# A mixer block's first stage: TensorE in a written order, whole modulations, one load queue

## The chip, the cores and the metric

The kernel runs on one core of one Trainium2 chip. TensorE (PE in the profile) multiplies matrices, VectorE (DVE), ScalarE (ACT) and GpSimd (POOL) work on elements, SyncE (SP) mostly issues transfers; ACT and POOL can issue transfers too. The metric is the device time of one execution in microseconds (us). Before the change it is 1306.2 us, the median of 3 runs (1304.97 to 1307.42).

## The reference

One layer of a diffusion block over 512 latent tokens with 2048 channels, and 256 context tokens. The input is normalised and modulated by a shift and a scale that come from a conditioning vector; one wide projection feeds an attention branch and a Fourier branch; both are gated, projected, merged and added to the input.

```python
shift, scale, gate = jnp.split(silu_c @ w_ada[l] + b_ada[l], 3, axis=-1)
h = _modulate(_rmsnorm(xs, norm_g[l]), shift[:, None], scale[:, None])
p = h @ w_l                      # q, k, v, z_a, u_b, z_b, g_a, g_b
...
y_a = (attn * jax.nn.silu(z_a)) @ w_pa
y_b = (_fourier_mix(u_b) * jax.nn.silu(z_b)) @ w_pb
out = xs + gate[:, None] * ((g_a * y_a + g_b * y_b) @ w_o)
```

`_fourier_mix` is the real part of a two-dimensional FFT over the tokens and over the 128 channels of each of four groups. All is float32; the kernel multiplies in a reduced float32 by writing each operand as a high and a low half and taking three products.

## The kernel before

The channels are cut into 16 input blocks of 128 (`kb` 0 to 15). x is held transposed (`xt`, channels by tokens).

**First stage** (lines 453 to 653). It computes the Fourier branch's two inputs: u_b, four tiles of 128 channels (tiles 0 to 3), and z_b, four more (tiles 4 to 7), each by 512 tokens. For every input block it needs three things:

- a *modulation* (`modulation`, L584): the block's 128 shifts and 128 scales, a product of the conditioning vector with 2 MB of `w_ada`, loaded in two halves of 1 MB (tag `wada`, four buffers, so two blocks). The product runs in four strips of 32 columns of TensorE (`matvec`, L527; the rows of line 534, 32 records to a modulation), ACT copies it out (`ado`, L542), TensorE transposes it twice (L545), DVE sums it to columns (L551) and makes `shift` and `gain` (L590, L591);
- the *rows* of the modulated input (`make_h`, L519): DVE multiplies by the gain and the norm (L521), ACT adds the shift and rounds to the high half (L522), DVE takes the low half (L523);
- the block's *weights* (`w_start`), loaded in pieces of up to 512 KB (`STEPS`, L41: one block with eight tiles for blocks 0 to 3, then two blocks with four tiles) and split into halves by ACT and DVE (`split_piece`, L254, whose two instructions are lines 177 and 178). Four raw buffers and three pairs of halves hold them; two more raw buffers (`mr`) serve from block 8 on.

A tile's product with a block is three matmuls (`mm3`, L326: high by high, line 328; high by low, line 329; low by high, line 330). The u tiles add up over all blocks in four PSUM banks of their own and are copied out once at the end; the z tiles go piece by piece through two other banks and are added on DVE into `part` (`keep`, L564; ACT for block 0). `start_work` (L559) is a generator that issues these products. The loop at L612 issues a modulation, the rows, then products that are due. The order of instructions on each engine is not the written one: a scheduler with a cost model of its own places what is ready, except inside `manual_schedule`, where the written order holds, and with `issue_after`, which keeps an instruction behind a given one on its engine. Before, only the modulations from block 3 on are inside `manual_schedule`, each for itself.

From block 8 on `form_row` (L601) makes two further forms of the input rows for the later products.

*Loads.* x, the first pieces and the modulations 0 to 2 are issued by SP; modulations from block 3 on by POOL (L462); the later pieces and the transform's tables by ACT (`asks`), at blocks given by `ASK`; pieces are split at blocks given by `SPLIT`.

**Transform** (lines 655 to 727). The Fourier mix is matrix products: `channels` with a table of 128 by 256 (`fch`), `positions` with tables of sines and cosines (`fsq`, two halves of 512 KB raw). The tables are split into halves after the first stage, `halves` forms sums and differences of u, `gate_b` applies SiLU to z, and each `positions` result is multiplied into z. The last four products of the first stage (z tiles, blocks 12 to 15) are issued in the same stretch.

**Afterwards** come the other projections, in products of a seven-product scheme (`Group`), attention, the branch projections and the output projection. Their weights come through the same queue of pieces: `get` (L287) hands out the next and splits as many ahead as `look` says, 4 from the end of the first stage, bounded by the pairs of halves (three, and two more from the group's second product, Q5).

Of the kernel before, what the change touches and what calls it, by code (L numbers as in the profile page):

```python
# [18 lines left out]
P = 128  # L19
# [24 lines left out]

ASK, SPLIT, MORE_RAW = (*range(1, 9), 9, 9, 10, 10, 11, 12), (*range(2, 13), 14), 8
# [75 lines left out]
def block_kernel(ctx, tc, xT, ctx_rows, ctx_toks, x, c_row, w_ss, w_gate, vecs, qkg, rope, dft_c, dft_s,  # L121
# [76 lines left out]
    def start_load():  # L198
# [12 lines left out]
        for p, src in zip(free, e.parts):  # L211
            raw = p[0].tile([P, 1024], F32, tag=p[2], bufs=p[3], name=uid("wr"))[:, : e.cols]
            asks[0].dma_start(raw if len(src.shape) == 2 else raw.rearrange("p (i j c) -> p i j c", i=4, j=2), src)
            e.raws.append((p, raw))
# [7 lines left out]
    may, asks = [0], [nc.sync]  # L222
# [134 lines left out]
    for p in start_pieces():  # L357
        if p[2:5:2] == (KK - 4, 4):
            for q in range(2):
                stream(("dfts", q), dft_s[:, q], 1024, 2, "raw")  # L360
            stream(("dftc", 0), dft_c, 256, 1, "raw")
        stream(("start", p), w_start[p[0] : p[0] + P * p[1]].rearrange("(p c) -> p c", p=P), p[1], p[2 + 1])
# [94 lines left out]
    mr, mrp = region("mr")  # L457
    xt = pap.tile([P, KK, T], F32, name="xt")

    def wada_load(kb, h):  # L460
        w = pap.tile([P, 8, 256], F32, tag="wada", bufs=4, name=uid("wa"))
        (nc.gpsimd if kb > 2 else nc.sync).dma_start(w, w_ss[kb, :, 8 * h : 8 * h + 8, :])  # L462
        return w

    for a, n in XCH:
        nc.sync.dma_start(xt[:, a : a + n, :], xT[:, a : a + n, :])


# [4 lines left out]
    nc.scalar.activation(ce, cvt, ACT.Exp, scale=-1.0)  # L473
    nc.scalar.activation(rt, ce[:, 0:1], ACT.Sqrt)
# [4 lines left out]
                            ce.rearrange("p (j k) -> p j k", j=2), op=ALU.mult)  # L479
    def token_norms():  # L480
# [30 lines left out]
    wada = {(0, h): wada_load(0, h) for h in range(2)}  # L511
    may[0] = 3
    load_more()
    wada.update({(1, h): wada_load(1, h) for h in range(2)})
    may[0] = 1
    load_more()
    asks[0] = nc.scalar

    def make_h(hi, lo, src, rr, kb, j):  # L519
        tmp = src  # L520
        first = nc.vector.scalar_tensor_tensor(tmp, src, gain[:, kb, j : j + 1], rr, op0=ALU.mult, op1=ALU.mult)  # L521
        act = nc.scalar.activation(hi, tmp, ACT.Identity, bias=shift[:, kb, j : j + 1])  # L522
# [36 lines left out]
    def start_work():  # L559
# [7 lines left out]
        for p in start_pieces():  # L567
            kb, nk, t, nt = p[2:]
            if (kb, t) == (KK - 4, 4):
                yield 0  # L570
# [1235 lines left out]
```

## Time and profile before

| | |
|---|---|
| median of 3 runs | 1306.2 us (1304.97 to 1307.42) |
| profiled execution | 1305.55 us, of which the span of the profile is 1303.3 us |
| granted TensorE clock, mean | 0.998 |
| busy: PE, PEld, DVE, ACT, POOL | 1279.5, 1047.4, 995.1, 685.4, 180.6 us |
| first matmul of the first stage's tiles | 23.47 us from the start |
| first matmul of the first product after the transform | 169.39 us |
| bytes moved | 318.54 MB, mean 244 GB/s |

The profile is one execution. Times run from the start of its span. A row of the timeline gives the start, the length, the engine, the line of the kernel, the operation, output and inputs by the names in the program, the shape, the count, and in brackets how long the engine had been idle and what released it. A matmul's row is longer than its share of the array, since matmuls overlap: what counts is the distance between starts. PEld is the weight load, which overlaps the matmul. A name such as `s` stands for a slot tile (rows of the input), `whi` and `wlo` for the halves of a weight piece, `pb` for the banks of the u tiles and of the transform, `pc` for those of the z tiles, `pd` for those of the modulations.

### The profile page before, as it was taken

The page shows a single profiled execution, that of the slowest core. Times are in us where ns is not written, and L with a number is a line of the kernel's source. Part 1 is how long each engine was busy: PE and PEld are TensorE (multiplying, and loading weights), DVE is VectorE, ACT ScalarE, POOL GpSimd, SP SyncE. Part 2 cuts the span into 40 slices and gives each one's busy share as a digit, 9 for nine tenths or more (in the row PEclk, how much of TensorE's full clock was granted, in tenths as well). Part 3 has the DMA queues.
Part 4 walks back from the last instruction along what each step waited for, and adds up shares of the span by engine and source line. Part 5 has one row for each costly group of instructions (what it writes and reads, how often), then busy time and mean ns, then how long its engine had stood idle before and what let it go on. Part 6 is the DMA issues. An engine that isn't in the chain of part 4 may idle for free.

```text
span 1303.3 us, 17544 instructions
## 1 busy us (share of the span) xinstructions
PE 1279.5 (98%) x6522; PEld 1047.4 (80%) x6522; DVE 995.1 (76%) x1295; ACT 685.4 (53%) x1079; POOL 180.6 (14%) x244
## 2 busy tenths in 40 slices
PE   6999999999999999999999999999999999999997
PEld 3577888888888888888888888888888888888885
DVE  4666899979688887657687766688798867887676
ACT  5222655555556465444254554666666646464544
POOL 0110011110202111011021010011110212221210
PEclk9999999999999999999999999999999999999999
DMA  9898487887899988976879897468872899998985
GB/s 382 338 373 349 178 244 183 242 243 255 209 284 260 265 287 271 292 209 179 273 200 267 294 224 258 169 221 245 251 230 82 236 246 250 244 212 232 220 205 173
DMA packets 103718, 318.54 MB, mean 244 GB/s; under 512 B 9808, under 2 KB 33104, under 8 KB 99280
## 3 DMA queue, kind: packets, MB, share of 16 engines
q0 software_dynamic: 30288, 123.75, 40.4%
q1 hardware_dynamic: 48720, 163.65, 35.3%
q10 hardware_dynamic: 24624, 30.02, 6.6%
q8 instruction: 51, 0.84, 0.2%
q14 instruction: 35, 0.29, 0.1%
HBM read 283.30 MB, written 34.09 MB: 244 GB/s over the span
## 4 chain that ended last, share of the span: by engine, by line
PE 91%; DMA 3%; DVE 2%; ACT 2%; issue 1%; SPq 0%; ACTq 0%; DVEq 0%
PE banks L328 10%; PE banks L329 10%; PE banks L330 10%; PE x L328 9%; PE x L330 9%; PE x L329 9%; PE y L329 7%; PE y L328 7%; PE y L330 7%; PE pd L534 2%; PE banks L1294 2%; PE pb L328 2%; PE pb L330 2%; PE pb L329 2%; DMA wa<-in_w_ss 1%; PE pc L328 1%
## 5 line engine op out<-in xcount | busy, mean ns | idle before, releaser
L177 ACT ACTIVATE whi<-R 128x1024 fp32r<-128x1024 f32 x138 | 145.2, 1059 | 140.2 <-PE banks L330 47.3
L178 DVE TENSOR_TENSOR wlo<-R,whi 128x1024 fp32r<-128x1024 f32 x138 | 167.5, 1221 | 55.4 <-ACT whi L177 55.2
L178 DVE TENSOR_TENSOR wlo<-wr,whi 128x1024 fp32r<-128x1024 f32 (+1 forms) x123 | 148.5, 1212 | 63.4 <-ACT whi L177 63.2
L177 ACT ACTIVATE whi<-wr 128x1024 fp32r<-128x1024 f32 (+1 forms) x123 | 128.8, 1051 | 116.6 <-PE y L330 37.4
L328 PE MATMUL banks<-whi,s 128*128 128x512 f32 x396 | 157.1, 397 | 2.2 <-DVE ev L862 1.5
L330 PE MATMUL banks<-whi,s 128*128 128x512 f32 x396 | 155.2, 392 | 0.0
L329 PE MATMUL banks<-wlo,s 128*128 128x512 f32 x396 | 155.1, 392 | 0.0
L328 PE MATMUL x<-whi,s 128*128 128x512 f32 x352 | 137.2, 390 | 0.0
L330 PE MATMUL x<-whi,s 128*128 128x512 f32 x352 | 137.0, 389 | 0.0
L329 PE MATMUL x<-wlo,s 128*128 128x512 f32 x352 | 137.0, 389 | 0.0
L328 PE MATMUL y<-whi,s 128*128 128x512 f32 x316 | 123.1, 389 | 0.4 <-DVE cxe L1015 0.4
L329 PE MATMUL y<-wlo,s 128*128 128x512 f32 x316 | 123.1, 390 | 0.3 <-DVE wlo L178 0.3
L330 PE MATMUL y<-whi,s 128*128 128x512 f32 x316 | 122.8, 389 | 0.0
L281 POOL DMA_DIRECT2D R<-in_w_g x64 | 55.9, 874 | 420.2 <-DVE wlo L178 247.5
L177 ACT ACTIVATE s<-wr 128x512 fp32r<-128x512 f32 (+2 forms) x93 | 60.4, 676 | 68.6 <-DMA wr<-cf_d 21.8
L178 DVE TENSOR_TENSOR s<-wr,s 128x512 fp32r<-128x512 f32 (+2 forms) x93 | 66.8, 749 | 31.7 <-ACT s L177 30.9
L328 PEld LDWEIGHTS banks<-whi,s 128*128 128x128 f32 x396 | 74.4, 188 | 17.7 <-ACT whi L177 1.9
L330 PEld LDWEIGHTS banks<-whi,s 128*128 128x128 f32 x396 | 74.4, 188 | 15.5
L329 PEld LDWEIGHTS banks<-wlo,s 128*128 128x128 f32 x396 | 74.4, 188 | 14.0 <-DVE wlo L178 0.2
L330 PEld LDWEIGHTS x<-whi,s 128*128 128x128 f32 x352 | 66.1, 188 | 13.8
L329 PEld LDWEIGHTS x<-wlo,s 128*128 128x128 f32 x352 | 66.1, 188 | 13.6
L328 PEld LDWEIGHTS x<-whi,s 128*128 128x128 f32 x352 | 66.1, 188 | 13.6
(293 smaller groups left out, 2829.4 us busy)
## 6 DMA issues: line engine op xcount, KB each, us to landing
wr<-in_w_g SPq DMA_DIRECT2D x128, 512.0 KB, 5.2
R<-in_w_g POOLq DMA_DIRECT2D x64, 512.0 KB, 7.5
wa<-in_w_ss POOLq DMA_DIRECT2D x26, 1024.0 KB, 8.2
R<-in_w_g SPq DMA_DIRECT2D x32, 512.0 KB, 5.6
wr<-in_w_gate SPq DMA_DIRECT2D x32, 512.0 KB, 5.1
wr<-in_w_o SPq DMA_DIRECT2D x24, 512.0 KB, 7.7
R<-in_w_o POOLq DMA_DIRECT2D x24, 512.0 KB, 9.5
wr<-in_w_pab SPq DMA_DIRECT2D x20, 512.0 KB, 6.4
```

The costliest lines, as they stand in the source:

```text
L177: first = nc.scalar.activation(hi, src, ACT.Copy)
L178: return first, nc.vector.tensor_tensor(lo, src, hi.bitcast(F32), op=ALU.subtract)
L281: nc.gpsimd.dma_start(chain[e.pc], e.nxt, accum_op=ALU.add)
L328: nc.tensor.matmul(o, ah, bh, start=start, stop=False, skip_group_check=cont)
L329: nc.tensor.matmul(o, ah, bl, start=False, stop=False, skip_group_check=cont)
L330: nc.tensor.matmul(o, al, bh, start=False, stop=stop, skip_group_check=cont)
L534: last = nc.tensor.matmul(acc[32 * j : 32 * j + 32, :256], c2[:, 8 * h + k, :], w[:, k, :], start=n < 4, stop=n >= KK - 4)
L1294: nc.tensor.transpose(tp[:, k * P : (k + 1) * P], p[:, k * P : (k + 1) * P], ident)
```

## The change

- All of TensorE's instructions from the norms to the transform's last tile stand in `manual_schedule`. Each modulation is written whole between two tiles: for blocks 0 to 3 two tiles, the next modulation, two tiles, its transposes, four tiles; then two modulations to a pair of blocks. The copy (ACT) is issued with the modulation (`modulate`), the transposes and the columns later (`columns`); the gain is made before the shift.
- Within a piece of two blocks the u tiles go by block first, then by tile. Where a piece has eight tiles, u and z tiles alternate (`TURNS`).
- All loads of the stage are issued by SP, chained in the written order (`ask`, `load_start`): after a modulation is written, the one two blocks later (three for the first) and the next piece are asked for. POOL and ACT issue none of them. The two raw buffers `mr` are gone; `ASK`, `SPLIT` and `MORE_RAW` too. Before the second modulation's load stand two pieces instead of three.
- The first sine table (`fsq0`) and the channel table (`fch`) have tiles beside `part`, are loaded before block 12's first piece and split after block 13's rows, in the loop's turn `kb == 10`. The second sine table is split after the stage.
- Each split of a piece, and each `form_row`, is kept behind the rows of the block at which it stands. The sums and differences of u are kept behind the last additions to the first z tiles.
- One, two and three of the next pieces are split between the transform's tiles; `look` is 2 after the transform and 4 from Q5 of the first group on.
- The square-root function is first called on a constant right behind the exponential.

The diff, cut to its core:

```diff
-ASK, SPLIT, MORE_RAW = (*range(1, 9), 9, 9, 10, 10, 11, 12), (*range(2, 13), 14), 8
+TURNS = (0, 4, 1, 5, 2, 6, 3, 7)
...
+        if p[2:5:2] == (KK - 4, 0):
+            stream(("dfts", 0), dft_s[:, 0], 1024, 2, "raw")
             stream(("dftc", 0), dft_c, 256, 1, "raw")
+        elif p[2:5:2] == (KK - 4, 4):
+            stream(("dfts", 1), dft_s[:, 1], 1024, 2, "raw")
...
-    def wada_load(kb, h):
-        w = pap.tile([P, 8, 256], F32, tag="wada", bufs=4, name=uid("wa"))
-        (nc.gpsimd if kb > 2 else nc.sync).dma_start(w, w_ss[kb, :, 8 * h : 8 * h + 8, :])
-        return w
...
+    def ask(q, *a):
+        with ExitStack() as line:
+            if last_load[0] is not None and q is nc.sync:
+                line.enter_context(tc.issue_after(last_load[0]))
+            ins = q.dma_start(*a).ins
+        if q is nc.sync:
+            last_load[0] = ins
...
+    def load_start():
+        may[0] = 1
+        with tc.issue_after(last_load[0]):
+            load_more()
+        assert not may[0]
+        last_load[0] = asked[0].ins
...
+    for n in range(len(XCH)):
+        load_x(n)
+    wada = {0: wada_load(0)}
+    for _ in range(2):
+        load_start()
+    wada[1] = wada_load(1)
+    load_start()
...
+    def modulate(kb):
+        two[kb] = bank2()
+        for h in range(2):
+            matvec(kb, h)
+        o = o_of[kb] = pap.tile([P, 256], F32, tag="ada_o", bufs=2, name=uid("ado"))
+        wada.pop(kb)
+        return nc.scalar.copy(o, two[kb][:, :256])
...
+            order = [[(i, k) for k in range(nk)] for i in range(nt)]
+            if t == 0 and nk > 1:
+                order = [[(i, k)] for k in range(nk) for i in range(nt)]
+            elif nt == 8:
+                order = [order[i] for i in TURNS]
...
+    with tc.manual_schedule(engines={mybir.EngineType.PE}):
+        norms = token_norms()
+        modulate(0)
+        wada[2] = wada_load(2)
+        load_start()
+        columns(0)
+        ins = make_h(0)
+        nc.scalar.copy(rx, rx0[0])
+        split_next()
+        with behind(ins):
+            split_next()
+            split_next()
+        for kb in range(4):
+            some(2)
+            modulate(kb + 1)
+            if kb < 3:
+                wada[kb + 3] = wada_load(kb + 3)
+                load_start()
+            some(2)
+            columns(kb + 1)
+            ins = make_h(kb + 1)
+            with behind(ins):
+                split_next()
+            if kb == 3:
+                some(2)
+                modulate(5)
+                for k in (6, 7):
+                    wada[k] = wada_load(k)
+                    load_start()
+                some(2)
+                columns(5)
+                make_h(5)
+            else:
+                some(4)
+        for kb in range(4, KK - 2, 2):
+            n = 3 if kb < KK - 4 else 2
+            for i in range(2):
+                k = kb + 2 + i
+                some(n)
+                modulate(k)
+                if k + 2 < KK:
+                    wada[k + 2] = wada_load(k + 2)
+                    for _ in range(2 if k + 2 == KK - 3 else 1):
+                        load_start()
+                some(2 - i)
+                columns(k)
+                ins = make_h(k)
+                with behind(ins):
+                    split_next()
+                    if k >= 8:
+                        form_row(k - 8)
+                if k == KK - 2:
+                    load_start()
+            some(n - (n == 2))
+            with behind(ins):
+                if kb == KK - 6:
+                    split_table(0)
+                    split_from(get(("dftc", 0)), fch[:, 0, :], fch[:, 1, :])
+                    load_start()
+        some(8)
...
-    for q in range(2):
-        split_from(get(("dfts", q)).rearrange("p (m n) -> p m n", m=2), fsq[:, 0, q], fsq[:, 1, q])
-    raw = get(("dftc", 0))
-    split_from(raw, fch[:, 0, :], fch[:, 1, :])
-    for g in range(4):
-        halves(g)
+    ordered = ExitStack()
+    ordered.enter_context(tc.manual_schedule(engines={mybir.EngineType.PE}))
+    for n in range(4):
+        next(work)
+        if n < 2:
+            with behind((finals[-1],)):
+                halves(2 * n)
+                halves(2 * n + 1)
...
         positions(g)
         if g < 2:
             channels(g + 2)
+        with behind((finals[-1],)):
+            for e in ahead[:g]:
+                split_piece(e)
+    ordered.close()
+    look[0] = 2
...
             if (g, name) == (0, "Q5"):
                 hl_pools += range(MORE_HL)
+                look[0] = 4
```

`some(n)` issues the next n steps of `start_work`, each a tile of a piece (a tile and a block for the u tiles of a two-block piece); `behind(ins)` is `issue_after` for several instructions.

More of the change, by code (lines that the diff above doesn't have):

```diff
@@ L509, in spread @@
         return acc
[L511 to L522, printed above, removed]
-        second = nc.vector.scalar_tensor_tensor(lo, tmp, shift[:, kb, j : j + 1], hi.bitcast(F32),
-                                                op0=ALU.add, op1=ALU.subtract)
-        return first, second, act
```

199 lines of the change are left out of this document (92 added, 107 removed).

## The prediction

> **What bounds the kernel now.** I read the page first, then a table of stretches with the edges put where TensorE changes its kind of work, then TensorE's own timeline in the first stretches.
>
> ```profile
> span 1303.3 us, 17544 instructions
> ...
> 0.00:23.47 23.47, 13.32 (x64) 6.53 (x65) 11.64 (x28) 15.10 (x27) 1.90 (x11) 1.00 0.93 368
> 23.47:63.00 39.53, 38.97 (x269) 23.37 (x270) 23.29 (x42) 10.16 (x17) 5.56 (x10) 1.00 0.91 357
> 63.00:137.95 74.95, 74.90 (x567) 52.92 (x567) 49.24 (x99) 22.13 (x32) 8.61 (x16) 1.00 0.86 337
> 137.95:169.39 31.44, 31.18 (x204) 28.49 (x204) 29.23 (x46) 19.64 (x31) 0.54 (x1) 1.00 0.57 205
> 169.39:400.00 230.61, 230.61 (x1020) 191.01 (x1019) 200.79 (x240) 128.72 (x223) 33.86 (x38) 1.00 0.86 241
> ```
>
> The stretch rows give the stretch, its length, then busy time and count for PE, PEld, DVE, ACT and POOL, the granted clock, the DMA share and GB/s. They are: the load of x and the norms; the input blocks 0 to 5; blocks 6 to 15; the end of the first stage with the transform; and the first of the products that follow. TensorE looks full in all but the first, but busy time says little here (a matmul's row is 0.39 us long while the next starts 0.23 us after it), so I count instructions. In the last row 1020 matmuls take 230.61 us, 0.2261 us each: nothing to gain there. For the stage itself I need the pitch of its matmuls, of a modulation, and of one that is cut:
>
> ```profile
> 48.13 0.40 PE L330 MATMUL pc<-s,wlo 128*128 128x512 f32 x1
> 48.46 0.62 PE L534 MATMUL pd<-wa,c 128*32 128x256 f32 x2
> 49.01 0.50 PE L328 MATMUL pc<-s,whi 128*128 128x512 f32 x1
> 49.35 0.40 PE L329 MATMUL pc<-s,whi 128*128 128x512 f32 x1
> ...
> 49.91 1.06 PE L534 MATMUL pd<-wa,c 128*32 128x256 f32 x12
> ...
> 51.79 1.48 PE L534 MATMUL pd<-wa,c 128*32 128x256 f32 x18
> ...
> 59.87 1.93 PE L534 MATMUL pd<-wa,c 128*32 128x256 f32 x30
> ...
> 88.23 0.39 PE L330 MATMUL pc<-s,wlo 128*128 128x512 f32 x1
> 88.55 1.93 PE L534 MATMUL pd<-wa,c 128*32 128x256 f32 x32
> 90.42 0.50 PE L328 MATMUL pc<-s,whi 128*128 128x512 f32 x1
> 90.75 0.40 PE L329 MATMUL pc<-s,whi 128*128 128x512 f32 x1
> 91.22 0.38 PE L545 MATMUL pd<-ident,ado 128*128 128x128 f32 x2
> 91.67 0.39 PE L329 MATMUL pc<-s,whi 128*128 128x512 f32 x1
> ...
> 163.03 0.28 PE L329 MATMUL pb<-fch,uh 128*128 128x256 f32 x1
> 163.15 0.28 PE L330 MATMUL pb<-fch,ul 128*128 128x256 f32 x1
> ```
>
> The pitch of a plain matmul I take as 0.2275 us (between the steady 0.2261 above and the 0.23 to 0.24 between starts here). A whole modulation (32 records) costs 88.23 to 90.75, 2.52 us, less two pitches: 2.07 us. The two transposes cost 91.22 to 91.67, 0.45, less one pitch: 0.22; with the short step into them I use 0.25. Now count. The stretch 23.47 to 63.00 holds 269 records: five modulations (160), ten transposes, so 99 matmuls. Ideal: 99 x 0.2275 + 5 x 2.07 + 5 x 0.25 = 34.1 us, measured 39.5: **5.4 us lost**. The stretch 63.00 to 137.95 holds ten modulations and 227 matmuls: 51.6 + 23.2 = 74.8 against 74.95, 0.1 lost. In 137.95 to 169.39 there are 144 matmuls of the transform (four times 12 and 24), which start 0.12 apart (163.03, 163.15), and 60 others: 13.7 + 17.3 = 31.0 against 31.44, 0.5 lost (about the wait quoted further down). So at most 6.0 us (0.46%) can be won between 23.47 and 169.39, and the start before that is bound by transfers at 0.93 of the DMA engines.
>
> **The change part by part.**
>
> *Whole modulations.* Modulations 1 to 5 are cut today, the later ones are whole. Two are cut 16 + 16 (1.07 us each by their rows below), two 2 + 30, one 2 + 12 + 18.
>
> ```profile
> 25.28 1.07 PE L534 MATMUL pd<-wa,c 128*32 128x256 f32 x16
> 27.66 1.07 PE L534 MATMUL pd<-wa,c 128*32 128x256 f32 x16
> ```
>
> A cut of two records costs 48.13 to 49.35, 1.22 us, less two pitches, 0.76 us, all of it extra, since the 30 left take the same 1.93 as 32. Halves cost 2 x 1.07 - 1.93 = 0.21 and one more entry and exit, each 0.1 (88.23 to 88.55 and 90.42 to 90.75 against 0.2275): 0.42. The 12 + 18 cost 1.06 + 1.48 - 1.93 + 0.21 = 0.82. Sum: 2 x 0.42 + 3 x 0.76 + 0.82 = **3.9 us** that a whole modulation saves. Six extra pieces in all.
>
> The Trainium skill ("TensorEngine Tiling (Array Packing)", section Key Properties) says that a change of tiling mode drains TensorE; a modulation works in strips of 32 columns and the rest in the full array, so it would charge each extra piece two drains. If the drains, the 0.21 us of entry and exit, were all that a cut costs, six would be worth 1.3 us and not 3.9. The trace charges more, because the 2-record rows are 0.62 long where two of 32 should be 0.12.
>
> *The written order's own waits.* TensorE now takes tiles, modulation and transposes as written, so where a scheduler today fills a wait with another tile, it will stand. Of the 5.4 us lost, 1.5 are waits that exist already (5.4 - 3.9). New ones come from this chain (DVE, ACT and PE rows of block 4, and of block 0):
>
> ```profile
> 23.45 0.75 DVE L523 SCALAR_TENSOR_TENSOR s<-xt,shift,s 128x512 fp32r<-128x512 f32 x1 [0.33 <-ACT s L522]
> 23.47 1.20 PE L328 MATMUL pb<-s,whi 128*128 128x512 f32 x4 [0.30 <-ACT s L522]
> ...
> 45.83 0.38 PE L545 MATMUL pd<-ident,ado 128*128 128x128 f32 x2
> 46.31 0.17 DVE L551 TENSOR_REDUCE adr<-pd 128x4 f32<-128x16 f32 x1 [1.35 <-PE pd L545]
> 46.98 0.75 DVE L521 SCALAR_TENSOR_TENSOR xt<-xt,gain,rx 128x512 f32<-128x512 f32 x1
> 47.76 0.43 DVE L607 TENSOR_TENSOR S<-xt 128x256 f32<-128x256 f32 x1
> 47.76 0.72 ACT L522 ACTIVATE s<-xt,shift 128x512 fp32r<-128x512 f32 x1 [3.32 <-DVE xt L521]
> 48.11 0.68 DVE L564 TENSOR_TENSOR part<-pc,part 128x512 f32<-128x512 f32 x1
> 48.71 0.74 DVE L523 SCALAR_TENSOR_TENSOR s<-xt,shift,s 128x512 fp32r<-128x512 f32 x1
> ```
>
> Row 0: its low half is ready at 23.45 + 0.75 = 24.2. The second matmul of a triple reads it and would start at 23.70. Today three more first products stand in (x4 at 23.47); in the written order it waits, 0.5 us. Rows 1 to 3: from the transposes (45.83) the high half is ready after 2.65 us (48.48) and the low half after 3.6 (49.45), 0.1 sooner with the gain now ahead of the shift. Behind the transposes four tiles are written, 12 x 0.2275 + 0.25 = 3.0 us, so the high half is in time and the low half, due at 3.2, is 0.3 late; an eviction (0.68) ahead of it on DVE makes it 0.6 to 1.0. I take 0.4 for each of three rows, 1.2, with 0.6 and 3 as ends. Block 0's four gate tiles run one after another through two banks that ACT empties; I take 0.4, with 0 and 1.2 (two evictions' worth at 0.6) as ends. From block 4 on the tiles of one block pair go by input block first, so that at least 3.7 us lie behind the transposes even for row 15 (one tile of 6, then four of 3: 0.25 + 15 to 18 matmuls); nothing, unless DVE is behind there.
>
> *One queue.* POOL's 26 transfers and ACT's 14 (11 pieces of weights, three of tables) go to SP, which is in no computing engine's way.
>
> ```profile
> 10.00:20.00 10.00, 9.22 (x47) 3.59 (x45) 6.37 (x11) 5.78 (x12) 0.00 (x0) 1.00 1.02 413
> ...
> wa<-in_w_ss POOLq DMA_DIRECT2D x26, 1024.0 KB, 8.2
> ...
> wr<-in_w_start ACTq DMA_DIRECT2D x11, 512.0 KB, 7.5
> ...
> 47.77 0.34 ACTq L213 DMA_DIRECT2D wr<-in_w_start  x1
> ...
> POOL wa L462 <- PE pd L534: 81.6, 25, 9.1
> ```
>
> From 10 to 20 us SP alone feeds the engines: 413 GB/s, so one queue carries the full rate. A modulation and a block of weights are 2 x 1.05 + 0.52 = 2.6 MB, 6.3 us at that rate; TensorE needs 8 x 3 x 0.2275 + 2.32 = 7.8 us a block. POOL waits for TensorE to free a buffer (81.6 us), not the reverse. Behind a waiting modulation load the start weights now queue, which before went by ACT; they are split a block ahead of use. The tight place is the fifth to seventh modulation, written closer together: laid out at these pitches from 23.47, the fifth has run at 57.7, the seventh's load can be issued then, lands some 8 to 9 us later behind 0.5 MB of weights, and is due at 67: no wait, slack about 1 us. ACT loses 14 issues of about 0.34 us, off the path. The first loads differ only in that one start piece (0.5 MB, 1.25 us) goes behind modulation 1, which so lands before its turn. The start stays at 23.47.
>
> *Tables in the tenth block.* One sine table and the channel table move ahead of the transform:
>
> ```profile
> 140.57 1.23 DVE L178 TENSOR_TENSOR fsq<-wr,fsq 128x1024 fp32r<-128x1024 f32 x1 [1.25 <-ACT fsq L177]
> ...
> 145.25 0.42 DVE L178 TENSOR_TENSOR fch<-wr,fch 128x256 fp32r<-128x256 f32 x1
> ...
> 154.89 0.39 PE L328 MATMUL pb<-fsq,ah 128*128 128x256 f32 x1 [0.26 <-DVE al L178]
> ```
>
> DVE was busy 29.23 of 31.44 us in the transform's stretch and loses 1.65 there. They land in the last short pair of blocks, which is 24 x 0.2275 + 2 x 2.32 = 10.1 us on TensorE; DVE's 49.24 us in 74.95 is 6.6 per 10.1, and with 1.65 and two form rows (0.43 each as at 47.76, today done earlier) 9.1. It fits with little over; I charge 0.3 for row 15 (0 to 1.2, one split). The wait at 154.89 comes from DVE being late with the split of the first transform product; the order there is written too, and all gate tiles now stand ahead of the transform instead of between: 0.4 again. The next weights are split between transform tiles, three pieces before the first product, as many as there are buffers now; the shorter look-ahead I charge nothing, because the split runs beside 2.7 us of matmuls a piece.
>
> **Sum.** Lost now 6.0; lost then 0.5 + 1.2 + 0.4 + 0.3 + 0.4 = 2.8, and about 0.1 in blocks 6 to 15. **Gain 3.1 us**, by ends from 0 (waits 3 + 1.2 + 0.5 + 1.2 = 5.9) to 5 (0.6 + 0.5). Behind 169.39 TensorE runs at its pitch, so an earlier start is carried to the end. The profiled execution took 1305.55 us (span 1303.3 and 2.25 around it), 0.65 under the median of 1306.2; it would be 1302.4, the median **1303.1**.
>
> **The rivals.**
>
> *DVE holds the stage (slower).* Rows are late by a whole split: a piece's split (1.04 on ACT, then about 1.2 on DVE) stands ahead of the low half in rows 1, 2, 3 and 15, 2.3 us each for 0.4 or 0.3. Then 9.2 - 1.5 = 7.7 more: 1310.8. It decides from 5.7 us more waiting on (3.1 + 2.6). For it: TensorE can no longer step aside, and DVE has most of the last pair full. Against: in the rows above the split follows the low half, and the change orders it so.
>
> *The transform is bound by DVE.* With 29.23 of 31.44 us busy DVE gives the earlier start back, all but the 0.5 us that its lighter load may leave: 1305.7. Against: TensorE waited only 0.5 there.
>
> *The loads.* Modulations 5 to 8 wait 1 us each for their weights, as slack runs out: 4 us more, 1307.1. Against: 6.3 us of loading for 7.8 of work.
>
> *Cuts are worth the mode changes alone*, 1.3: 2.6 less gain, 1305.7. Against: the 0.62 us rows. This is what the skill's sentence on drains alone would give.
>
> *No new waits.* The scheduler of the other engines puts the rows first, 5 to 6 us won: 1300.6.
>
> **How the numbers follow.** A measurement of this kernel tells about 0.2%, 2.6 us, from no change. Chances: forecast 0.43 (own range 1301.5 to 1305; 0.35 of it over 2.6 us faster, 0.08 within), no new waits 0.13 (faster), the transform 0.17 and cuts 0.04 (within), loads 0.09 (0.06 within, 0.03 slower), DVE 0.14 (slower). Faster 0.48, within 0.35, slower 0.17. The range goes from 1300 to 1308.5: it takes in all but the DVE case and the edge of the best.
>
> **What would show it.** Right: 32 records in each L534 row from the first block on, 3.5 us sooner at the sixth modulation for equal work, the first product (x, 169.39 now) near 166.3, the DMA page with no modulation load on POOL. Wrong: waits of TensorE for rows (L522, L523 of before) over 0.6 us a block, for wa landings, or for al. A loss that begins only after the first product would speak for the look-ahead, which I charged nothing.

## The result, and the profile after

The changed kernel takes 1308.6 us (median of 22 runs, 1306.94 to 1312.78) where the kernel before takes 1306.2 in the same rounds: the ratio is 1.002, with a 95% interval of 1.0012 to 1.0029. The prediction was 1303.1, a gain of 3.1 us; it became a loss of 2.4. The profiled execution took 1308.72 us, and these rows of its page say what changed in kind:

```profile
span 1306.9 us, 17539 instructions
...
wa<-in_w_ss SPq DMA_DIRECT2D x32, 1024.0 KB, 8.2
```

All 32 loads of modulation weights are in SyncE's queue, none in GpSimd's. The modulations are whole, from the first block on (TensorE's timeline, modulations 1 and 2):

```profile
25.77 1.93 PE L551 MATMUL pd<-wa,c 128*32 128x256 f32 x32
35.29 1.94 PE L551 MATMUL pd<-wa,c 128*32 128x256 f32 x32
```

So the change did what it says. Where the time went shows in the start of equal work. Rows of the table of stretches, with edges at the first input row, at the first product and at the same later product, of the kernel after, and then the answering stretches of the kernel before (start and end, length, busy time and count of PE, PEld, DVE, ACT and POOL, clock, DMA share, GB/s):

```profile
23.60:168.52 144.92, 141.69 (x1039) 104.42 (x1040) 98.91 (x185) 53.87 (x82) 0.71 (x1) 1.00 0.81 313
168.52:180.00 11.48, 11.48 (x51) 9.02 (x49) 6.36 (x8) 3.58 (x4) 0.55 (x1) 1.00 0.86 285
...
168.52:231.83 63.31, 60.63 (x262) 48.44 (x261) 58.19 (x70) 35.70 (x54) 10.00 (x12) 1.00 0.76 202
```

```profile
169.39:180.87 11.48, 11.48 (x53) 9.51 (x52) 10.83 (x12) 7.23 (x8) 1.45 (x2) 1.00 0.80 274
...
169.39:228.35 58.96, 58.96 (x263) 48.82 (x261) 58.07 (x69) 35.89 (x54) 9.97 (x12) 1.00 0.82 209
```

The stage from the first row to the first product took 145.92 us before (23.47 to 169.39) and takes 144.92 now: 1.0 won, where 3.1 were forecast. Behind the first product it takes 4.35 us longer to the same later matmul: the product that started at 228.35 before starts at 231.83 now, so a lead of 0.87 has become a lag of 3.48. From there to 419 us the lag does not move by 0.01, and at the last matmul it is 3.27. VectorE tells the two apart. Before, it is busy 58.07 of the 58.96 us from the first product to that later one, idle 0.89, and none of TensorE's matmuls there starts late. Now it does the same 58.2 us of work in 63.31, idle 5.12, and all of that in the first 11.48 us, of which it works 6.36 (10.83 before). So VectorE falls behind early. TensorE pays for it in two places, at 181 us (a row further down) and again at the end of the stretch, where splits come late:

```profile
222.52 0.50 PE L327 MATMUL x<-s,s 128*128 128x512 f32 x1 [0.41 <-ACT s L176]
...
223.59 0.50 PE L328 MATMUL x<-s,s 128*128 128x512 f32 x1 [0.34 <-DVE s L177]
...
227.60 0.50 PE L329 MATMUL y<-whi,s 128*128 128x512 f32 x1 [0.98 <-DVE s L177]
```

**The stage.** These are TensorE's waits in it of over 0.2 us (rows of its timeline with the idle time in front and who ended it):

```profile
24.39 0.51 PE L328 MATMUL pb<-s,whi 128*128 128x512 f32 x1 [0.28 <-DVE s L594]
...
33.16 0.50 PE L327 MATMUL pb<-s,whi 128*128 128x512 f32 x1 [0.58 <-ACT s L593]
33.95 0.51 PE L328 MATMUL pb<-s,whi 128*128 128x512 f32 x1 [0.28 <-DVE s L594]
...
43.24 0.50 PE L328 MATMUL pb<-s,whi 128*128 128x512 f32 x1 [1.20 <-DVE s L594]
...
51.64 0.50 PE L328 MATMUL pb<-s,whi 128*128 128x512 f32 x1 [0.28 <-DVE s L594]
...
123.47 0.50 PE L327 MATMUL pc<-s,whi 128*128 128x512 f32 x1 [0.60 <-DVE part L613]
```

The idle time in brackets counts from the modelled end of a matmul, so I go by starts against the pitch of 0.2275 us. Row 0 loses 0.56 us, row 1 1.47 in all (0.16 of it at 30.5), row 2 1.38, row 3 0.46, and block 13 0.76: 4.6 us. Behind rows 1 and 2 and block 13 stand the orders of VectorE and ScalarE:

```profile
29.13 1.23 DVE L177 TENSOR_TENSOR wlo<-wr,whi 128x1024 fp32r<-128x1024 f32 x1 [3.37 <-ACT whi L176]
30.27 0.17 DVE L576 TENSOR_REDUCE adr<-pd 128x4 f32<-128x16 f32 x1
...
31.90 0.59 ACT L611 COPY part<-pc 128x512 f32<-128x512 f32 x1 [0.38 <-PE pc L329]
32.38 0.72 ACT L593 ACTIVATE s<-xt,shift 128x512 fp32r<-128x512 f32 x1
...
41.84 0.69 DVE L613 TENSOR_TENSOR part<-pc,part 128x512 f32<-128x512 f32 x1 [0.50 <-PE pc L329]
42.45 0.74 DVE L594 SCALAR_TENSOR_TENSOR s<-xt,shift,s 128x512 fp32r<-128x512 f32 x1
...
120.61 1.22 DVE L177 TENSOR_TENSOR wlo<-wr,whi 128x1024 fp32r<-128x1024 f32 x1
121.74 0.28 DVE L577 TENSOR_SCALAR gain<-adr,bsc,small 128x2 f32<-128x2 f32 x1
```

In row 1 a weight split (29.13) runs ahead of the row's reduction (30.27), and then an eviction that itself waits for TensorE (31.90) goes ahead of the row's high half (32.38). In row 2 an eviction waits 0.50 us for the tile that TensorE is just ending, with the row's low half queued behind it. In block 13 a split of 1.22 us stands between the reduction and the gain.

**Behind the first product.** Here R is a raw piece of weights, and Z and S are the two forms of the input rows that `form_row` makes, which are split into halves here. ScalarE, VectorE, TensorE and GpSimd of the kernel after, each in order of time, and the times from issue to landing of the tile b_d's transfers (two stores here and two loads much later; the longest is the second store):

```profile
171.46 1.06 ACT L176 ACTIVATE whi<-R 128x1024 fp32r<-128x1024 f32 x1 [7.82 <-PE x L329]
176.58 0.38 ACTq L1007 DMA_DIRECT2D qr<-in_rope  x1
177.49 1.06 ACT L176 ACTIVATE s<-Z 128x1024 fp32r<-128x1024 f32 x1 [4.96 <-issue]
...
172.56 1.23 DVE L177 TENSOR_TENSOR wlo<-R,whi 128x1024 fp32r<-128x1024 f32 x1 [1.35 <-ACT whi L176]
178.58 1.23 DVE L177 TENSOR_TENSOR s<-Z,s 128x1024 fp32r<-128x1024 f32 x1 [3.54 <-ACT s L176]
...
181.00 0.50 PE L328 MATMUL y<-wlo,s 128*128 128x512 f32 x1 [0.94 <-DVE wlo L177]
...
169.73 0.55 POOL L803 DMA_DIRECT2D b_d<-part  x1 [6.01 <-DVE part L780]
...
DMA to landing us min/median/max: 3.3/3.5/6.7
```

ScalarE ends a split at 172.5 and does nothing for 5 us. What stands next in its queue is not a computation but the load of the rotation table into qr, issued at 176.58. The kernel before issues it at 169.59, as the transform ends:

```profile
169.59 0.33 ACTq L931 DMA_DIRECT2D qr<-in_rope  x1
...
170.45 2.01 ACT L177 ACTIVATE s<-Z 128x1024 fp32r<-128x1024 f32 x2 [2.82 <-PE pb L330]
```

The buffer qr lies where an earlier buffer has ended its life. Now that is part (bytes 202720 to 219104 of each partition; qr is at 204768), which the second store b_d<-part reads: issued at 169.73, landed 6.7 us later, at 176.4. Before, part lay higher (212960 to 229344), and qr over working buffers of the transform, which its last products read. These places are those of the built programs. It is the change that moved part: fch and the first half of fsq were added behind it in the same pool, which ends at a fixed place. The experiments test that reading.

### The profile page after: what moved, and what is told of

Its sections match the earlier page's. It is cut to its first block, busy times and chain, and to the rows that moved or that the text cites. A ratio compares the mean times of both kernels' runs of the same rounds, so it can differ in the third digit from the quotient of the medians.

```text
span 1306.9 us, 17539 instructions
## 1 busy us (share of the span) xinstructions
PE 1278.5 (98%) x6522; PEld 1046.7 (80%) x6522; DVE 993.8 (76%) x1296; ACT 684.4 (52%) x1080; POOL 166.4 (13%) x218
## 4 chain that ended last, share of the span: by engine, by line
PE 78%; DVE 9%; DMA 6%; issue 3%; ACT 3%; SPq 0%; ACTq 0%; POOL 0%; DVEq 0%; POOLq 0%
PE banks L327 10%; PE banks L328 10%; PE banks L329 10%; PE x L329 7%; PE x L328 7%; PE x L327 6%; PE y L329 6%; PE y L327 6%; PE y L328 5%; DVE wlo L177 3%; PE banks L1371 2%; PE pd L551 2%; DMA wr<-in_w_g 2%; DMA wr<-in_ctx_toks 1%; DVE s L177 1%
## 5 line engine op out<-in xcount | busy, mean ns | idle before, releaser
L177 DVE TENSOR_TENSOR wlo<-R,whi 128x1024 fp32r<-128x1024 f32 x138 | 167.6, 1221 | 58.7 <-ACT whi L176 58.3
L327 PE MATMUL x<-whi,s 128*128 128x512 f32 x356 | 138.9, 390 | 0.0
L329 PE MATMUL x<-whi,s 128*128 128x512 f32 x356 | 138.7, 390 | 0.0
L328 PE MATMUL y<-wlo,s 128*128 128x512 f32 x308 | 120.2, 390 | 0.9 <-DVE wlo L177 0.9
L329 PE MATMUL y<-whi,s 128*128 128x512 f32 x308 | 119.9, 390 | 1.0 <-DVE s L177 1.0
L327 PE MATMUL y<-whi,s 128*128 128x512 f32 x308 | 120.2, 390 | 0.4 <-DVE cxe L1091 0.4
```

The source lines that it names most:

```text
L177: return first, nc.vector.tensor_tensor(lo, src, hi.bitcast(F32), op=ALU.subtract)
L327: nc.tensor.matmul(o, ah, bh, start=start, stop=False, skip_group_check=cont)
L328: nc.tensor.matmul(o, ah, bl, start=False, stop=False, skip_group_check=cont)
L329: nc.tensor.matmul(o, al, bh, start=False, stop=stop, skip_group_check=cont)
```

## The experiments

Leads are given against the kernel before, by the start of the same matmul. "Lost behind" is the change of the lead from the first product (169.39 before) to the product of 228.35. "Idle" is VectorE's idle time between the two, the length of the stretch less its busy time in it (before: 58.96 - 58.07 = 0.89).

| kernel | stage, us | lead at first product | lost behind | VectorE idle | median, us | ratio to before, 95% |
|---|---|---|---|---|---|---|
| after | 144.92 | 0.87 | 4.35 | 5.12 | 1308.6 | 1.0012 to 1.0029 |
| e1, tables in front of part | 144.93 | 0.06 | 1.78 | 2.44 | 1307.04 | 0.9985 to 1.0016 |
| e2, look-ahead 4 | 144.89 | 0.89 | 4.31 | 5.09 | 1309.39 | 1.0012 to 1.0032 |
| e3, rope load by GpSimd | 144.91 | 0.75 | 0.80 | 1.64 | 1306.79 | 0.9989 to 1.0013 |
| e4, e1 and e2 | 144.91 | 0.94 | 1.29 | 1.95 | 1306.12 | 0.9988 to 1.0014 |
| e5, e4 and five cuts | 148.64 | -3.47 | 1.32 | 1.94 | 1310.27 | 1.0011 to 1.0036 |
| e6, e4 and the rows' orders | 142.79 | 3.03 | 1.30 | 1.94 | 1304.60 | 0.9973 to 1.0000 |
| e7, e4 and Z first | 144.95 | 0.77 | 2.39 | 2.48 | 1307.40 | 0.9989 to 1.0016 |
| e8, e6 and Z first | 143.53 | 2.21 | 2.39 | 2.47 | 1306.94 | 0.9985 to 1.0021 |
| e9, before and Z's low halves twice | 145.90 | -0.12 | 1.27 | 0.94 | 1307.42 | 0.9994 to 1.0018 |
| e10, e6, splits alternating, rope by GpSimd | 142.91 | 3.01 | 1.26 | 1.98 | 1303.69 | 0.9976 to 0.9994 |
| e11, e10 and a gate's load later | 142.82 | 2.53 | 1.24 | 1.99 | 1306.27 | 0.9996 to 1.0013 |
| e12, before and that load later | 145.85 | 0.0 | 0.0 | 0.89 | 1310.35 | 1.0019 to 1.0041 |

### Layout or look-ahead (e1 to e4)

Two things changed behind the first product that could hold ScalarE up: the memory under qr, and look[0] = 2. Each is undone alone, the wait is moved to another engine, and both are undone together.

e1, only the order of three allocations:

```diff
-    part = ppool.tile([P, NS, T], F32, name="part")
+    fch = ppool.tile([P, 2, 256], F32R, name="fch")
+    fsq = [ppool.tile([P, 2, 2, T], F32R, name="fsq0")]
+    part = ppool.tile([P, NS, T], F32, name="part")
...
-    fch = ppool.tile([P, 2, 256], F32R, name="fch")
-    fsq = [ppool.tile([P, 2, 2, T], F32R, name="fsq0")]
```

> The changed kernel with fch and fsq0 allocated in front of part, so that part lies at the top of memory again and the qr buffer of the rope load overlays fsq0 (read last by the products of positions) in place of part (read last by the second b_d store). Every engine's order stays that of the changed kernel. Theory A (the layout: ScalarE's rope load waits for that store, and the splits behind it come late): the rope load is issued near 170 us in place of 176.58, ScalarE's idle 4.96 us ahead of s<-Z goes, the waits of y at 179.55 (1.44 us) and of 221 to 228 (2.9 us) go or shrink to those of before, the lead of 0.87 us at the first product is kept to the end, and the run takes 1304.5 to 1305.5 us by the changed kernel's 1308.6. Theory B (the shorter look-ahead, 2 in place of 4, puts the splits in an order that comes late): the rope load is early here too, but the loss behind 179 us stays within 1 us of 4.1 and the time within 1 us of 1308.6.

e2, look-ahead alone:

```diff
-    look[0] = 2
+    look[0] = 4
     fn.close()
```

> The changed kernel with the look-ahead kept at 4 behind the transform, the layout left as it is. Theory A: ScalarE's rope load still waits for the second b_d store until about 176.5 us, the loss behind 179 us stays, at 3 to 5 us, and the time at 1307.5 to 1309.5. Theory B: the two splits of wr that come earlier in ScalarE's order cover the wait, the loss goes, and the run takes 1304.5 to 1305.5 us.

e3, in load_rotations:

```diff
-        nc.scalar.dma_start(turning, rope)
-        nc.scalar.dma_start(new_q()[:, 0, 0:2, :], rows)
+        nc.gpsimd.dma_start(turning, rope)
+        nc.gpsimd.dma_start(new_q()[:, 0, 0:2, :], rows)
```

> The changed kernel with the two loads rope and rows issued by GpSimd in place of ScalarE, look-ahead 2, layout left as it is. Theory A: it is GpSimd that waits for the store now, ScalarE goes straight on to s<-Z near 172 us, the waits of 179 to 187 us go, and the time is 1304.5 to 1306.5 us (up to a microsecond more than with the layout mended, where GpSimd's own work behind the load is late). Theory B: the order of the splits is the same, the waits of 221 to 228 us stay, and the time is 1307.5 to 1309.

e4 has the edits of e1 and e2.

> Both: the tables in front of part, and the look-ahead kept at 4. Theory A: no more than 0.5 us from the run with the layout mended alone, so 1304 to 1306 us. Theory B: as the run with look-ahead 4 alone. Should both matter, this run alone reaches 1304.5 to 1305.5, and each of the others lies between it and 1308.6.

With the layout put right, the 3.54 us in which VectorE waited for the split of Z are gone. Its waits of over 0.3 us from 169 to 185 us in e1:

```profile
173.36 1.23 DVE L177 TENSOR_TENSOR wlo<-R,whi 128x1024 fp32r<-128x1024 f32 x1 [1.35 <-ACT whi L176]
184.25 1.23 DVE L177 TENSOR_TENSOR wlo<-R,whi 128x1024 fp32r<-128x1024 f32 x1 [0.45 <-ACT whi L176]
```

and in e2, look-ahead 4 with the layout left as it is:

```profile
172.54 1.23 DVE L177 TENSOR_TENSOR wlo<-R,whi 128x1024 fp32r<-128x1024 f32 x1 [1.35 <-ACT whi L176]
178.53 1.23 DVE L177 TENSOR_TENSOR wlo<-R,whi 128x1024 fp32r<-128x1024 f32 x1 [3.51 <-ACT whi L176]
```

In e3 it is GpSimd that waits, and the view of qr there (160 to 185 us) names what for, the landing of the store:

```profile
L1007 POOL DMA_DIRECT2D qr<-in_rope x1: 532/532/532, 176.4 to 176.4; - x1
...
  DMA b_d<-part: 6.0, 1
```

e1 issues the rope load at 172.28 and loses 1.78 us behind the first product in place of 4.35, with every engine's order unchanged; e3, which leaves the layout and the look-ahead alone but lets GpSimd do the waiting, loses 0.80. e2 loses 4.31. So the rope load's wait is the main cause, and the shorter look-ahead is not: alone it changes nothing. Beside the mended layout it may be worth up to half a microsecond (1.29 in e4 by 1.78); the medians of e1 and e4 lie 0.9 apart with overlapping intervals, so I leave its size open. Theory A's times were too good, by 1.5 us for e1, 0.3 for e3 and 0.1 for e4. e1's profile starts 0.8 us later from the load of x (24.39 by 23.60), which none of this touches, and a loss remains, 1.8 us in e1, 1.3 in e4 and 0.8 in e3. In all three VectorE still waits 1.35 us for a split whose buffers the first product must free; why e3 loses least was not taken apart. Both mends together give back the loss of the change, no more.

### The price of a cut (e5)

```diff
-            for h in range(2):
-                matvec(kb, h)
+            matvec(kb, 0, (0,))
+            some(1)
+            matvec(kb, 0, range(1, 8))
+            matvec(kb, 1)
...
```

This is done for modulations 6 to 10 of e4, where no row is waited for.

> The kernel with both mends (tables in front of part, look-ahead 4), and modulations 6 to 10 cut again into 2 records, one tile, 30 records (first the two halves' first matmul, as the order of before had it). No wait of rows stands in these blocks, so the price of a cut shows in the start of the first product alone (168.44 us in the kernel with both mends, counted from the first row's start at 23.53, so 144.9). The prediction's price, 0.76 us a cut, sets it 3.8 us later; the price of two changes of mode alone, 0.21 a cut, 1.05 us later. If one cut record costs no more than its own 0.06 us and an exit, 0.3 to 0.5 a cut, 1.5 to 2.5.

```profile
69.91 0.39 PE L329 MATMUL pb<-s,wlo 128*128 128x512 f32 x1
70.23 0.62 PE L551 MATMUL pd<-wa,c 128*32 128x256 f32 x2
70.78 0.50 PE L327 MATMUL pb<-s,whi 128*128 128x512 f32 x1
...
172.86 0.40 PE L327 MATMUL x<-whi,s 128*128 128x512 f32 x1
```

From its first row at 24.22 to the first product at 172.86 the stage takes 148.64 us, 3.73 more than in e4: 0.75 us a cut, where the prediction had 0.76 and its rival of mode changes alone 0.21. That price stands; the other cuts of the kernel before (16 + 16 and 12 + 18, 1.7 of the 3.9 us) were not made again. What the change wins by whole modulations is real; it is spent elsewhere.

### The rows' orders (e6)

```diff
+        with behind(hold.get((kb, t), ())):
             if kb == 0 or t < 4:
                 nc.scalar.copy(dst, acc)
...
             ins = make_h(kb + 1)
+            if kb < 3:
+                hold[kb, 6 if kb == 0 else 7] = ins
...
                 with behind(ins):
-                    split_next()
+                    for _ in range({KK - 4: 0, KK - 3: 2}.get(k, 1)):
+                        split_next()
```

behind(...) around an instruction puts it after the given ones in its engine's order. The weight load that follows modulation 13 goes behind its splits as well, since it needs the buffer that they free.

> The kernel with both mends, and three orders of VectorE and ScalarE mended: the third gate eviction of block 0 behind row 1's high half on ScalarE, the last eviction of blocks 1 and 2 behind the low half of rows 2 and 3 on VectorE, and the weight split that stood inside row 13's chain behind it (one weight load goes behind it with it). The waits of row 1 (0.99 and 0.55), row 2 (1.38) and block 13 (0.75) fall to 0.3 each or nothing, and the stage from the first row to the first product takes 142 to 143 us by 144.9. If an earlier first product is carried to the end, the run is 2 to 2.8 us faster than with both mends (1306.1). If VectorE holds the stretch behind it (59.7 of 60.6 us busy from 169.4 to 230 in the kernel before), half or more of that is given back by 230 us, and the run is 0.5 to 1.3 us faster.

```profile
33.10 0.50 PE L328 MATMUL pb<-s,whi 128*128 128x512 f32 x1 [0.29 <-DVE s L594]
...
41.50 0.50 PE L328 MATMUL pb<-s,whi 128*128 128x512 f32 x1 [0.29 <-DVE s L594]
...
123.23 0.50 PE L329 MATMUL pb<-s,wlo 128*128 128x512 f32 x1 [0.26 <-DVE wlo L177]
...
166.36 0.40 PE L327 MATMUL x<-whi,s 128*128 128x512 f32 x1
```

Each row now costs about 0.5 us (row 0 0.56, rows 1 to 3 0.52, 0.49, 0.49, block 13 0.42: 2.5 in place of 4.6), and the stage takes 142.79 us, 2.1 less than in e4. Of the 3.03 us of lead at the first product 1.30 are lost behind it, as e4 loses 1.29 of 0.94. The stretch is 60.26 us long in both. So it does not eat a lead because it is a lead: VectorE starts earlier with TensorE there, what is lost does not depend on when the stretch begins, and the 2.1 us are passed on whole. The expectation that half of them would be given back was wrong.

The median, 1304.60, is 1.5 us under e4 and 1.6 under the kernel before, the edge of what can be told. The profiled run, 1308.89, is the slowest of its twelve and not typical. It loses its time at 537 us: TensorE waits there for a weight split that stands behind the split of a context row, whose load lands late, and then the clock goes (stretch rows, columns as above):

```profile
535.00:538.00 3.00, 1.02 (x4) 0.29 (x2) 2.90 (x4) 1.97 (x4) 0.00 (x0) 0.97 0.61 168
538.00:544.00 6.00, 5.29 (x12) 4.13 (x13) 4.41 (x6) 3.85 (x6) 0.00 (x0) 0.50 0.91 309
```

### The order of the splits (e7, e8, e10) and VectorE's room (e9)

e7 puts both splits of Z ahead of the split that waits for buffers; e8 is e6 with the same edit:

```diff
+    for h in range(2):
+        forms["Z5"][4 * h : 4 * h + 4] = split_form(whole["Z5", h])
+        z_done.append(z_last[0][0])
     load_rotations(qkg[:, 0:2, :])
...
-                w = get((name, self.g, pc))
+                with behind(z_done if (self.g, name) == (0, "P1") else ()):
+                    w = get((name, self.g, pc))
```

> The kernel with both mends, and ScalarE's two splits of Z put ahead of the weight split that waits for a free pair of buffers until the first product has read its own (171.4 us). If VectorE's idle time of 1.7 us between 171 and 175.3 is what turned a lead of 0.94 us at the first product into 0.32 behind at 225, that idle time goes (under 0.5), no wait of over 0.3 us stands at 220 to 225, and the lead at 230 is 0.5 to 0.9. If the order of the splits at 215 to 225 is the cause, the waits there (1.9 us) stay.

> The two edits before together: first product as with the rows' orders mended, 2 to 2.8 us earlier than with both mends alone. If VectorE holds the stretch behind it and has no idle time left there, most of the lead at the first product (3 us on the kernel before) is lost by 230 us where VectorE's own work does not start earlier, and the run is at 1304 to 1305; if not, at 1302.5 to 1303.5.

VectorE's waits behind the first product of e7 (168.62):

```profile
175.38 1.23 DVE L177 TENSOR_TENSOR wlo<-R,whi 128x1024 fp32r<-128x1024 f32 x1 [0.66 <-ACT whi L176]
178.10 1.23 DVE L177 TENSOR_TENSOR wlo<-R,whi 128x1024 fp32r<-128x1024 f32 x1 [1.49 <-ACT whi L176]
```

Against the expectation the two make 2.15 us, 0.57 more than the waits that e4 has there (1.35 and 0.23): the weight splits come one for each quarter of a product that TensorE ends, and with Z out of the way nothing is left to fill the time between them. The loss grew to 2.39, in e7 and in e8; VectorE's work in the stretch is 0.6 us more as well (58.9 by 58.3), since another subtraction now falls into it. e8's stage lost another 0.8 us at a modulation that waited for its second half at 68.6. Its median, 1306.94, lies above both times that were expected, and its profiled run, 1315.30, is the slowest of its twelve.

e10 takes e6 and writes the order out: Z, weights, Z, weights, S, S, weights, with the rope load issued by GpSimd as in e3. The second Z is split after the second piece of the first product is fetched, and the fetches that follow stand behind it.

> The kernel with both mends and the rows' orders, and ScalarE's order behind the first product written so that VectorE always has a split to subtract: Z, weights, Z, weights, S, S, weights, with the rope load issued by GpSimd. VectorE's idle time between the first product and 224 us falls from 1.6 to 0.8 or less, the waits at 218 to 225 (1.3 us) go, and the lead over the kernel before is 2.3 to 3 us at 230 (1.75 with the rows' orders alone). But in all kernels looked at the load of a context row lands at 533 to 534.5 us whatever the lead, so the lead is lost again at 537, and the run takes 1303.5 to 1305.

```profile
170.43 1.23 DVE L177 TENSOR_TENSOR wlo<-R,whi 128x1024 fp32r<-128x1024 f32 x1 [0.21 <-ACT whi L176]
...
179.49 1.23 DVE L177 TENSOR_TENSOR wlo<-R,whi 128x1024 fp32r<-128x1024 f32 x1 [0.58 <-ACT whi L176]
```

The first two waits shrink (to 0.21 and 0.36), two others take their place (0.58 and 0.63): 1.98 us idle, 1.26 lost, as without the edit. That step failed. Yet e10 has the lowest median of all: 1303.69 us, 0.9985 of the kernel before (0.9976 to 0.9994), 4.9 us under the changed kernel. Unlike in e6's profile, the lead also gets past 537: the split of the context row runs at 531.89, 2.5 us sooner than in e6's profile, and the lead at the last matmul is 2.24. In e10 the second rope load, which falls into that time, comes from GpSimd as well. Whether this makes the difference to e6 was not tried apart, and the difference itself (0.9 us of the median) is not shown, since the two intervals overlap.

e9 asks how much room VectorE has in the kernel before:

```diff
         split_from(src, hi, lo)
+        if turn_fm[0] <= 8:
+            nc.vector.tensor_tensor(lo, src, hi.bitcast(F32), op=ALU.subtract)
         return rows4(hi, lo)
```

> The kernel before, with the low halves of the two splits of Z computed twice: 2.3 us more of VectorE's work right behind the first product, the same result. If VectorE holds the stretch from 169.4 to 230 us (59.7 of 60.6 us busy there, idle 0.65 between the first product and 224), TensorE comes 1.7 to 2.4 us later to the products of 230 us than in the kernel before, and the run takes 1307.5 to 1308.6. If TensorE holds it and VectorE runs beside it, under 0.3 us later and no measurable change.

```profile
169.51:229.74 60.23, 59.67 (x263) 48.58 (x261) 59.29 (x70) 35.98 (x54) 10.29 (x12) 1.00 0.77 199
```

The stretch of e9, columns as above: of the 2.3 us of added work 1.2 shows in VectorE's busy time here (59.29 by 58.07), the rest has been put off behind it, and the stretch is 1.27 us longer, with VectorE idle 0.94 as before. The expectation was 1.7 to 2.4, so there is a microsecond that VectorE can put off; what it cannot put off costs its full length. By the end of the profile 0.5 is left of it, and the medians don't tell it from no change. In all kernels but e7, e8 and e9 the stretch holds 58.1 to 58.3 us of VectorE's work, so the loss is its idle time beyond 0.9 plus at most 0.3 of work. That is arithmetic and doesn't say which engine holds the stretch; e9 does, and so do the waits: in every kernel that loses time there, TensorE's late starts end with a split of VectorE or ScalarE. So VectorE sets the length of the stretch in those kernels. In the kernel before and in e12 no start is late, TensorE sets it, and VectorE is about a microsecond short of doing so.

### A load moved at 520 us (e11, e12)

```diff
-           + [(5, "P1", 1), (5, "Q5", 1), (5, "P2", 1), (5, "Q6", 1), (5, "P7", 1),
+           + [(5, "Q5", 1), (5, "P2", 1), (5, "Q6", 1), (5, "Q6", 3), (5, "P7", 1),
...
```

> The same, with one gate's weights (0.5 MB) taken out from between the loads of the two context rows and asked for later in the same group. The second context load lands 1.2 to 1.7 us earlier, the wait at 535 to 538 us falls under 0.3, the granted clock keeps 1.00 there (0.50 from 538 to 544 in the profile with the rows' orders), the lead of 230 us reaches the end, and the run takes 1301.5 to 1303.5. If it is not this load that sets 537, the time stays that of the kernel without the move.

> The kernel before with the same move of one gate's weights, as a control. It waits 0.67 us at 537 itself, so it gains at most 0.7 us: 1305.5 to 1306.2.

```profile
638.28 0.50 PE L328 MATMUL y<-whi,s 128*128 128x512 f32 x1 [1.24 <-DVE cxe L1015]
```

The row is TensorE's in e12. The wait at 537 went, in the kernel before too (e12 leads by 0.29 us behind it, and by 1.00 at 624), but the load that was put off now crowds the same group's later ones: in e12 a context row lands at 630.5 us in place of 627.2. TensorE waits at 633 to 638 us in both kernels, 3 us in all, and both lose more than the move wins: 1306.27 us where 1301.5 to 1303.5 were expected, and 1310.35 where 1305.5 to 1306.2 were. The expectations had followed one end of the queue alone.

## Why the prediction was wrong

**The cuts: right as far as measured.** 3.9 us for modulations 1 to 5, at 0.76 a small piece; measured 0.75.

**The written order's waits: the right mechanism, two terms mis-sized.** Forecast for rows 1 to 3: 1.2, measured 3.3; for block 13 nothing ("nothing, unless DVE is behind there"), measured 0.76. Against that row 15 (0.3) and al (0.4) did not come, and of block 0's evictions (0.4) only the 0.16 that is counted with row 1. Together 4.6 by 2.8, which is most of the 2.1 us that the stage fell short. The step that failed here is "I take 0.4 for each of three rows", and with it the ground given against the first rival, "the split follows the low half, and the change orders it so". The change puts a split behind the row before it. Nothing keeps it out of the next row's chain, nor an eviction that waits for TensorE from ahead of the half that TensorE waits for. So the first rival's mechanism was there, at rows 1 and 13, for 1 us or less each and not the 2 of its price. With those orders mended (e6) the waits are 2.5 us and the first product starts at 166.36; the prediction had it near 166.3. That the two agree so closely is partly luck: rows at 0.5 each and 0.42 for block 13 stand in for terms that did not come.

**"Behind 169.39 TensorE runs at its pitch, so an earlier start is carried to the end": half wrong, and this turned the sign.** In the kernel before TensorE does run at its pitch there, and a lead is carried: e6 hands on to the product of 228.35 all of the 2.1 us that it gained on e4. But the sum had no term for a loss that begins there, and 4.35 us were lost. This is the step that failed by most. 2.6 of them, by e1, are the rope load's wait for the store that reads part, and 3.6 by e3, where the splits also come in another order. The prediction followed the tables in time, to which stretch of VectorE they move, and never in memory, to what lies below them then. Three questions would have found it: which load now writes where a store still reads, on which engine does it wait, and who stands behind it.

**"I charge nothing" for the shorter look-ahead: right within half a microsecond.** The prediction added that a loss behind the first product would speak for the look-ahead. It did begin there, and e2 cleared the look-ahead.

**One queue: right.** No modulation waits for its weights in the profile after. **The tables in the tenth block: right on the time** (they fit, no wait at al), wrong in the memory.

**The transform bound by VectorE**, the rival at 0.17, had the engine right and the place wrong: in the kernel after VectorE sets the time from 169 to 230 us and not ahead of it. In the row of the prediction that covers it, 169.39 to 400, it is busy 200.79 of 230.61 us, 87%; the row was read for TensorE alone, and over too long a stretch to show the first 60.

**The sum:** 1.0 won in the stage and 4.35 lost behind it are 3.35, the lag of 3.48 less the 0.13 us by which the first row starts later; forecast were 3.1 won and nothing lost. (The two profiled executions lie 3.17 us apart, the medians 2.4.)

## What to carry to other kernels

An allocation that moves is a dependency that moves: when buffers change pools, list what now lies where the next buffers come, whose last reader may be a store that takes 6.7 us to land, and which engine's queue stands behind the load that waits for it. Give such loads to an engine with nothing urgent behind them. Where one engine gets a written order, the others' orders must be written at the same places, since a scheduler that no longer moves the first engine's work can still put a ready split or eviction ahead of the late one that all wait for; and gains of two microseconds can be won or lost again at every later place where a transfer lands just in time.

## What the hardware showed that was not expected

TensorE's two waits ahead of the stretch at clock 0.50 in e6's profile:

```profile
536.58 0.49 PE L327 MATMUL y<-whi,s 128*128 128x512 f32 x1 [1.05 <-ACT whi L176]
538.72 0.80 PE L328 MATMUL y<-wlo,s 128*128 128x512 f32 x1 [1.64 <-DVE wlo L177]
```

The matmul ahead of them started at 535.14, so the starts lie 1.44 and 2.13 us apart. The granted clock fell to 0.50 at 537.85, while the second wait was still on, and stayed there for 6.83 us: the following matmuls started 0.43 us apart in place of 0.23. With the two gaps the lead of 1.73 us became a lag of 3.65. e8's profile has the same pair of waits (starts 1.46 and 2.13 us apart, the last at 540.66) and then the clock at 0.50 for 3.41 us, from 541.54 on; later one gap of 4.48 us between starts, ending at 923.24, is followed by 3.41 us at 0.50 as well. A single wait of 1.6 us in the stage (41.64 to 43.24 in the kernel after) left the clock at 1.00.

The Trainium skill ("TensorE: Matmul & The Clock Gate", Part 1: The HAM clock gate) says that the clock falls to half after an idle window of about 3.4 us. The gap of 4.48 us agrees. The pairs go further: no gap in them is that long, and in the 3.41 us ahead of each fall (534.44 to 537.85 in e6, 538.13 to 541.54 in e8) TensorE still started five matmuls, about 1.1 us of work. So two shorter gaps close together can do it; how much work would have kept the clock up, no run here shows.
